# Splitting projection weights on VectorE instead of GpSimd during the delta rule, and the output residual in half rows

## The chip, the cores and the metric

The kernel runs on one core of a Trainium2 chip. The metric is the device time of one execution in microseconds (us), of which the median of several executions is taken. The profile writes PE for TensorE's matmuls and PEld for its weight loads, DVE for VectorE, ACT for ScalarE, POOL for GpSimd and SP for the engine that issues most DMAs.

## The reference, cut to what matters

One layer of a streaming encoder. A prompt of 2048 tokens and a sample of 32 tokens are normalised, projected by one wide matrix, and go through two branches:

```python
hp = layer_norm(x_prompt, ln0_g, ln0_b)                 # 2048 x 1024; the sample has 32 rows
qa, ka, va, za, qkv_b, zb, a_b, b_b, gate_a, gate_b = split_projection(hp @ w_in)
ya = (chunk_band_attention(qa, ka, va, rel_bias) * silu(za)) @ w_branch_a
ob, s_new = gated_delta_rule(q, k, v, g, beta, s0)      # after a conv of qkv_b, chunks of 64 tokens
yb = (rmsnorm(ob) * gdn_norm_w * silu(zb)) @ w_branch_b
mix = sigmoid(gate_a) * ya + sigmoid(gate_b) * yb
y = layer_norm(ALPHA * hp + mix @ w_out, ln_g, ln_b)
```

All values are fp32. To get nearly fp32 results out of fp16 matmuls, the kernel splits each operand into a high part (rounded to fp16) and a low part (what the rounding left over), and adds up three products: high by high, high by low, low by high. The change concerns where the low parts of `w_in` are formed, and the term `ALPHA * hp` of the last line, the residual.

## The kernel before, in words

**Stages.** The tokens go through in two halves of 1024 (the second with the 32 sample rows). For each half the wide projection is cut into 49 jobs of 128 columns each. A job's weights are 1024 x 128, in SBUF as a 128x1024 tile `wraw`. The first jobs of a half feed branch B, the delta rule; the following ones feed branch A, the attention. After the second half comes the merge: branch matmuls (`a<-ghi,whi` and its two companions in the profile), the gates `sg`, the output projection (`pj<-woh,mh`, `b<-woh,mh`), the residual tile `xt` and the last norm. In the profiled execution the delta rule's recurrence runs from about 217 to 510 us and again from about 1013 to 1307 us; the merge fills the time from 1661 us to the end.

**Who sets the order.** The program is written by generators ("streams") that a small planner runs in order of a planned clock: class `Flow` gives each instruction a price, and whichever stream has the earliest clock writes its next instruction. The result is one fixed list of instructions for each engine, which the chip works off in that order; an instruction that waits holds back all behind it on its engine. `flow.spend(key, cost)` moves a stream's clock on, and charges an engine's planned time, without an instruction. A price that differs from the real duration changes no instruction, only where it stands.

**A weight job.** `fetch` loads `wraw` (two buffers, `raw_gate`). `divide` (below, in `trunk`) makes the two fp16 tiles `whi` and `wlo` (two buffers each, `w_gate`). In half 0 it first finds a power of two that scales the weights: ACT squares the tile into `whi` and sums it into `w_sq`; PE adds that up over partitions (`b<-w_sq,tiny`); DVE, POOL (a `pow`) and DVE turn it into `w_scale`. In both halves ACT then writes the scaled weights back into `wraw` (`wraw<-wraw,w_scale`, 128x1024), casts them to `whi` in two halves of 512, and POOL forms `wlo` as the difference `wlo<-wraw,whi`, in two instructions of 512. `multiply` then runs 48 matmuls for a job in half 0 (two blocks of 8 x 3) and 72 in half 1: `pj<-hi,whi`, `pj<-hi,wlo`, `pj<-lo,whi`.

**The delta rule.** DVE is the engine with the most instructions here. `substitute` inverts triangular systems step by step in pairs of small instructions, `sys_t` and `sys_u`, two systems at a time. `chain` carries the state from chunk to chunk: PE `x<-state,k_bd`, DVE `r`, PE `x<-r,u_bd`, DVE `vn`, PE `x<-vn,kd_bd`, DVE `state`, two token blocks at a time. `conv` does the width-4 convolution as three `acc<-raw,cwT,acc` instructions of 128x512 on DVE. Their matmuls stand on PE between the `pj` matmuls of the weight jobs.

**The order of the jobs** is made by `all_jobs`: `HEAD` gate jobs, the job "ab", the list `ORDER` (16 jobs of branch B with 5 gate jobs between them), `TAIL` = 6 gate jobs, 16 jobs of branch A, and the remaining gate jobs.

**The merge.** PE is the bound: for each 256 tokens 16 branch products go through three `a` banks; DVE multiplies each with its gate (`sg<-sg,a`), adds pairs (`sg<-sg`), ACT makes the high part `mh`, DVE or POOL the low part `ml`, and the output projection follows. `x_load` prepares the residual of each 128 rows, `finish` adds the projection to it (`xt<-pj,xt`, `xt<-b,xt`), takes the statistics and applies the norm (`xt<-xt,m,lng`, `xt<-xt,m,lnb`). `x_load` first makes (x - mean) * rstd on DVE (`xt<-xt,mv`, 128x1024), then multiplies by the row `l0g` and adds the row `l0b` (128x1024 each), on DVE for the first two tiles and on POOL for the other fifteen.

Of the kernel before, what the change touches and what calls it, by code (L numbers as in the profile page):

```python
# [15 lines left out]
AF = mybir.ActivationFunctionType  # L16
ALU = mybir.AluOpType
# [32 lines left out]
HEAD, TAIL = [2, 3], [6, 6]  # L50
# [5 lines left out]
ORDER = [(0, 0), (0, 1), (0, 2), None]  # L56
# [212 lines left out]
def trunk(ctx: ExitStack, tc: tile.TileContext, x_p, x_s, cache_k, cache_v, st_conv, st_gdn,  # L269
          ln0_g, ln0_b, w_in, w_ab, rel_rev, conv_w, a_log, dt_bias, gdn_w, w_a, w_b, w_out,  # L270
          ln_g, ln_b, y_p, y_s, nk_p, nv_p, nc_p, ng_p, nk_s, nv_s, nc_s, ng_s):
    nc = tc.nc
    ctx.enter_context(tc.manual_schedule())
    flow = Flow()
    V = Engine(flow, nc.vector, "V")
    S = Engine(flow, nc.scalar, "S")
    G = Engine(flow, nc.gpsimd, "G")
# [3 lines left out]
    def dma(dst, src, eng=nc.sync):  # L281

        eng.dma_start(dst, src)  # L283
        size = 2 if dst.dtype == F16 else 4
        n = size
        for k in dst.shape:
            n *= k

        n = max(n, n // (size * dst.shape[-1]) * 768)
        return flow.transfer("SP" if eng is nc.sync else "S", n)  # L290
# [7 lines left out]
    def mark():  # L298
        return Mark(flow)
# [55 lines left out]
    mv = const.tile([P, SEQ // P + 1, 2], F32, name="mv")  # L355
# [215 lines left out]
    class Job:  # L571
# [3 lines left out]
        def __init__(self, half, wid, src, evac=None, key=None, cols=P, blocks=None):  # L575
            self.wid = wid
            self.half, self.src, self.evac, self.cols, self.key = half, src, evac, cols, key
            self.end = self.two = False
            self.blocks = blocks or BLOCKS[half]

    NRAW = 2
# [33 lines left out]
    def factors(wid):  # L615

        inv, half_ = w_inv[:, wid:wid + 1], w_half[:, wid:wid + 1]
        V.reciprocal(out=half_, in_=w_scale[:, wid:wid + 1])
        yield
        V.tensor_scalar(out=inv, in0=half_, scalar1=h_scale[:, 2:3], scalar2=None, op0=ALU.mult)  # L620
        V.tensor_scalar(out=half_, in0=half_, scalar1=h_scale[:, 3:4], scalar2=None, op0=ALU.mult)

    def divide():

        while True:
            job, raw, t = yield from q_raw.get()
            yield w_gate
            hi = wpool.tile([P, KD, P], F16, tag="whi", bufs=2, name="whi")
            lo = wpool.tile([P, KD, P], F16, tag="wlo", bufs=2, name="wlo")
            sc = w_scale[:, job.wid:job.wid + 1]  # L630
            yield t
            if job.half == 0:
                S.activation(out=hi[:], in_=raw[:], func=AF.Square, accum_out=w_sq[:])
                yield
                yield from power(sc, w_sq[:])
                flow.start(factors(job.wid))
            src, main = raw[:, :, 0:job.cols], hi[:, :, 0:job.cols]
            S.activation(out=src, in_=src, func=AF.Copy, scale=sc)
            for i in range(2):
                ks = slice(4 * i, 4 * i + 4)  # L640
                S.copy(out=main[:, ks], in_=src[:, ks])
                yield

                rest_ = lo[:, ks] if job.cols == P else hi[:, ks, job.cols:P]
                G.tensor_tensor(out=rest_, in0=src[:, ks], in1=main[:, ks], op=ALU.subtract)
                if i:
                    raw_gate.give()
                    q_w.put((job, hi, lo))
                yield
# [129 lines left out]

    rest = [[job_gate(half, br, f) for br in range(2) for f in range(KD)] for half in range(2)]  # L780
# [1138 lines left out]

    def all_jobs():  # L1920
        for half in range(2):
            for what in [None] * HEAD[half] + ["ab"] + ORDER:
                if what is None:
                    yield rest[half].pop(0)
                elif what == "ab":
                    yield Job(half, 48, [(0, w_ab[:, :, 0:NH]), (32, w_ab[:, :, NH:2 * NH])], key=(1, None, 0), cols=HD,
                              blocks=AB_BLOCKS[half])
                else:
                    p, i = what
                    wid = (16 + 4 * i if i < 3 else 28) + p  # L1930
                    yield Job(half, wid, [(0, w_in[wid])], key=(1, p, i))
            for _ in range(TAIL[half]):
                yield rest[half].pop(0)
            for p in range(NP):
                for i, f in enumerate((8, 4, 0, 12)):
                    yield Job(half, f + p, [(0, w_in[f + p])], key=(0, p, i))
            yield from rest[half]

    def marked():

        ahead, half = [], None
        for job in all_jobs():
            if job.half != half:
                if ahead:
                    ahead[-2].two = ahead[-1].end = True
# [12 lines left out]
        ahead[-2].two = ahead[-1].end = True  # L1958
        yield from ahead
# [200 lines left out]
    def x_ahead():  # L2160
        n = SEQ // P
        for gt in [*range(n - 2), n, n - 2, n - 1]:
            yield x_slots
            w = Rows()
            flow.start(x_load(w, gt, P if gt < SEQ // P else DEC))
            q_x[gt == SEQ // P].put(w)

    def x_load(w, gt, rows):
        w.ready, w.half_done = mark(), mark()
        w.xt = xt = fp.tile([P, D], F32, tag="xt", bufs=3, name="xt")  # L2170
        w.st = fp.tile([P, 2, 6], F32, tag="fst", bufs=3, name="fst")
        yield dma(xt[:rows], x_s if rows < P else x_p[gt * P:(gt + 1) * P, :])
        yield rows_ready
        V.tensor_scalar(out=xt[:rows], in0=xt[:rows], scalar1=mv[:rows, gt, 0:1],
                        scalar2=mv[:rows, gt, 1:2], op0=ALU.subtract, op1=ALU.mult)
        yield
        eng = V if gt < 2 else G
        eng.tensor_tensor(out=xt[:rows], in0=xt[:rows], in1=rowv["l0g"][:rows], op=ALU.mult)
        yield
        eng.tensor_tensor(out=xt[:rows], in0=xt[:rows], in1=rowv["l0b"][:rows], op=ALU.add)  # L2180
        w.ready.done()

    def finish(w, gt, rows, c, ps, end):
# [81 lines left out]
    rowv = {}  # L2265
# [42 lines left out]
```

## Time and profile before

| | us |
|---|---|
| median of 3 runs (lowest, highest) | 2088.36 (2082.26, 2091.96) |
| the profiled execution, its own time | 2083.65 |
| its span, first to last instruction | 2081.6 |
| PE busy in it | 1968.6 |
| DVE, ACT, POOL busy in it | 1499.7, 978.1, 633.1 |

The profiled execution is one run; its time is 4.7 us below the median of the three. Busy time of PE is an upper figure, since its matmuls are pipelined and their records overlap: a busy PE can still hold short waits. The rows of a group read: line, engine, operation, output<-inputs, shape, count | busy us, mean ns | idle time of the engine just before them, and what ended it. Nearly all instructions carry line 260, the helper that records them, so groups are told apart by the names of their tiles. A wait row reads: who waited <- for whom: us in total, times, longest.

### The profile page before, as it was taken

The numbers are of one execution on the slowest core, as the hardware profiler recorded it, in microseconds if no ns is written. First come the engines' busy times: TensorE is split into PE (matmuls) and PEld (weight loads), VectorE is DVE, ScalarE is ACT, GpSimd is POOL, SyncE is SP. The second block draws the span as 40 slices with busy tenths as digits, with TensorE's granted clock in tenths as the row PEclk, the third lists the DMA queues.
The fourth block names the chain that finished last, engine by engine and source line by source line (L and its number), as shares of the span: only waits on it lengthen the run. The fifth ranks groups of instructions, "written<-read, shape, count | busy, mean of one in ns | idle before, by whom it ended". The sixth has DMA issues, their size and how long they took to land. (4 is left out here: it accounts for less than half of the span.)

```text
span 2081.6 us, 41386 instructions
## 1 busy us (share of the span) xinstructions
PE 1968.6 (95%) x15098; PEld 1411.3 (68%) x15098; DVE 1499.7 (72%) x4661; ACT 978.1 (47%) x2098; POOL 633.1 (30%) x708
## 2 busy tenths in 40 slices
PE   4999999999999999998999999999999988999998
PEld 3454666766465657566667777667666777888996
DVE  7679889873377758679998986356656667666775
ACT  5565554444466667564544543355656641111110
POOL 6244333422312113243332331311011134433342
PEclk9999999999999999999999999999999999999999
DMA  3233232323423233122233233332232445433331
GB/s 119 72 92 106 75 102 57 100 80 91 116 86 111 70 92 100 65 85 72 66 89 83 77 99 84 105 92 76 72 88 88 129 137 175 132 102 122 102 116 54
DMA packets 197719, 196.49 MB, mean 94 GB/s; under 512 B 79622, under 2 KB 147570, under 8 KB 197516
## 3 DMA queue, kind: packets, MB, share of 16 engines
q1 hardware_dynamic: 197516, 193.85, 31.6%
q8 instruction: 119, 1.95, 0.4%
q14 instruction: 84, 0.69, 0.1%
HBM read 135.91 MB, written 50.53 MB: 90 GB/s over the span
## 5 line engine op out<-in xcount | busy, mean ns | idle before, releaser
L260 PE MATMUL pj<-hi,whi 128*128 128x512 f16 (+2 forms) x1992 | 644.8, 339 | 10.4 <-DVE zb L260 2.7
L260 PE MATMUL pj<-hi,wlo 128*128 128x512 f16 (+2 forms) x1952 | 635.9, 338 | 2.4 <-POOL wlo L260 2.3
L260 PEld LDWEIGHTS <-whi 128*128 128x128 f16 x3984 | 413.5, 105 | 214.5 <-issue 3.9
L260 PE MATMUL pj<-lo,whi 128*128 128x512 f16 (+2 forms) x1992 | 457.7, 340 | 0.0
L260 POOL TENSOR_TENSOR wlo<-wraw,whi 128x512 f16<-128x512 f32 x192 | 226.9, 1184 | 585.9 <-ACT whi L260 313.0
L260 PEld LDWEIGHTS <-wlo 128*128 128x128 f16 x1952 | 204.8, 105 | 111.1 <-issue 10.7
L260 ACT CAST mh<-sg 128x256 fp32r<-128x256 f32 x64 | 25.9, 406 | 279.6 <-DVE sg L260 279.6
L260 ACT CAST ph<-b 128x512 f16<-128x512 f32 (+2 forms) x224 | 93.1, 421 | 100.0 <-PE b L260 96.8
L260 DVE TENSOR_TENSOR pl<-b,ph 128x512 f16<-128x512 f32 (+2 forms) x224 | 107.7, 485 | 44.7 <-ACT ph L260 43.1
L260 PE MATMUL a<-ghi,whi 128*128 128x256 f32 (+1 forms) x512 | 132.6, 290 | 6.3 <-DVE sg L260 6.2
L260 DVE TENSOR_TENSOR sys_u<-sys_u,sys_t 128x60 f32<-128x60 f32 (+23 forms) x527 | 129.3, 251 | 6.7
L260 ACT ACTIVATE wraw<-wraw,w_scale 128x1024 f32<-128x1024 f32 (+1 forms) x98 | 111.5, 1138 | 46.6 <-DVE w_scale L260 42.9
L260 PE MATMUL a<-ghi,wlo 128*128 128x256 f32 (+1 forms) x512 | 130.3, 285 | 0.0
L260 ACT CAST whi<-wraw 128x512 f16<-128x512 f32 (+1 forms) x196 | 119.4, 612 | 20.9 <-PE pj L260 18.0
L260 DVE TENSOR_TENSOR sys_t<-sys_u,sys_p 128x60 f32<-128x60 f32 (+21 forms) x459 | 121.2, 265 | 6.1
L260 ACT ACTIVATE sb<-sb,mx,unit 128x640 f32<-128x640 f32 (+4 forms) x128 | 108.8, 851 | 20.0 <-DVE mx L260 19.7
L260 DVE SCALAR_TENSOR_TENSOR acc<-raw,cwT,acc 128x512 f32<-128x512 f32 x144 | 114.0, 792 | 5.4 <-ACT acc L260 4.4
L260 POOL TENSOR_TENSOR w_scale<-w_scale,mhalf 128x1 f32<-128x1 f32 x49 | 30.9, 631 | 269.3 <-DVE w_scale L260 204.2
L260 PE MATMUL b<-ident,sb 128*128 128x128 f32 x560 | 100.6, 279 | 5.3 <-ACT sb L260 2.2
L260 PEld LDWEIGHTS a<-ghi,whi 128*128 128x128 f32 x512 | 98.0, 191 | 9.0 <-DVE sg L260 7.8
L260 ACT COPY v_t<-o 128x64 f32<-128x64 f32 x132 | 27.7, 210 | 161.1 <-PE o L260 133.3
L260 PEld LDWEIGHTS a<-ghi,wlo 128*128 128x128 f32 x512 | 97.8, 191 | 0.3
(350 smaller groups left out, 4221.8 us busy)
## 6 DMA issues: line engine op xcount, KB each, us to landing
wraw<-in_w_in SPq DMA_DIRECT2D x192, 256.0 KB
sg<-sig SPq DMA_DIRECT2D x112, 128.0 KB
sig<-sig SPq DMA_DIRECT2D x44, 256.0 KB
sys_p<-sol_p SPq DMA_DIRECT2D x17, 512.0 KB
x<-in_x_p SPq DMA_DIRECT2D x16, 512.0 KB
xt<-in_x_p SPq DMA_DIRECT2D x16, 512.0 KB
out_y_p<-xt SPq DMA_DIRECT2D x16, 512.0 KB
glo<-g SPq DMA_DIRECT2D x14, 512.0 KB
```

The source lines that it names most:

```text
L260: r = f(*a, **k)
```

## The change

Jobs that run beside the delta rule get a mark, `delta`: all of `ORDER` and the first four of the six `TAIL` jobs in both halves, and the `HEAD` jobs of half 1: 25 jobs in half 0 and 28 in half 1, 53 of 96 with low parts. For them

- ACT no longer writes the scaled weights back. It makes each half of `whi` straight from the raw weights, with the scale (`whi<-wraw,w_scale`, 512);
- DVE forms the low part from the raw weights, `wlo = wraw * w_scale - whi`, in one instruction for each half, in place of POOL. The instruction is written past the planner's own wrapper, and its 0.7 us are charged to a key "W" which no engine has, so that the plan sees DVE as free;
- in half 0 the stream waits 1.0 us of planned time between ACT's square and the matmul of `w_sq`.

The other jobs keep the old way. In the merge, all residual tiles are done by DVE: (x - mean) * l0g, then that * rstd + l0b, each in two halves of 512 columns; POOL has none of them left.

```diff
             if job.half == 0:
                 S.activation(out=hi[:], in_=raw[:], func=AF.Square, accum_out=w_sq[:])
-                yield
+
+                yield flow.cur.clock + (1.0 if job.delta else 0.0)
                 yield from power(sc, w_sq[:])
                 flow.start(factors(job.wid))
             src, main = raw[:, :, 0:job.cols], hi[:, :, 0:job.cols]
-            S.activation(out=src, in_=src, func=AF.Copy, scale=sc)
+            if not job.delta:
+                S.activation(out=src, in_=src, func=AF.Copy, scale=sc)
             for i in range(2):
                 ks = slice(4 * i, 4 * i + 4)
-                S.copy(out=main[:, ks], in_=src[:, ks])
-                yield
 
                 rest_ = lo[:, ks] if job.cols == P else hi[:, ks, job.cols:P]
-                G.tensor_tensor(out=rest_, in0=src[:, ks], in1=main[:, ks], op=ALU.subtract)
+                if job.delta:
+
+                    S.activation(out=main[:, ks], in_=src[:, ks], func=AF.Copy, scale=sc)
+                    yield
+                    nc.vector.scalar_tensor_tensor(out=rest_, in0=src[:, ks], scalar=sc, in1=main[:, ks],
+                                                   op0=ALU.mult, op1=ALU.subtract)
+                    flow.spend("W", 0.7)
+                else:
+                    S.copy(out=main[:, ks], in_=src[:, ks])
+                    yield
+                    G.tensor_tensor(out=rest_, in0=src[:, ks], in1=main[:, ks], op=ALU.subtract)
...
-        V.tensor_scalar(out=xt[:rows], in0=xt[:rows], scalar1=mv[:rows, gt, 0:1],
-                        scalar2=mv[:rows, gt, 1:2], op0=ALU.subtract, op1=ALU.mult)
-        yield
-        eng = V if gt < 2 else G
-        eng.tensor_tensor(out=xt[:rows], in0=xt[:rows], in1=rowv["l0g"][:rows], op=ALU.mult)
-        yield
-        eng.tensor_tensor(out=xt[:rows], in0=xt[:rows], in1=rowv["l0b"][:rows], op=ALU.add)
+        for name, q, op0, op1 in (("l0g", 0, ALU.subtract, ALU.mult), ("l0b", 1, ALU.mult, ALU.add)):
+            for c in range(2):
+                cs = slice(c * 512, (c + 1) * 512)
+                V.scalar_tensor_tensor(out=xt[:rows, cs], in0=xt[:rows, cs], scalar=mv[:rows, gt, q:q + 1],
+                                       in1=rowv[name][:rows, cs], op0=op0, op1=op1)
+                yield
```

(The part left out gives the jobs in `all_jobs` their mark, and sets it to False when a job is made.)

Since the planner's clock moves, every engine's list is written anew: PE's has as many matmuls of each kind as before, in another order. Three places show what that means.

DVE in the delta rule of the second half, where a conv ends (`acc`, `qk_s`) beside two systems (`sys_t`, `sys_u`) and the state chain (`r`, `vn`, `state`). Before:

```order
L260 TENSOR_SCALAR vn<-x,sc 128x64
L260 TENSOR_TENSOR sys_u<-sys_u,sys_t 128x2x24
L260 TENSOR_TENSOR sys_u<-sys_u,sys_t 128x8
L260 SCALAR_TENSOR_TENSOR qk_s<-e,acc 128x32
L260 SCALAR_TENSOR_TENSOR state<-state,sc,x 128x64
L260 TENSOR_TENSOR sys_t<-sys_u,sys_p 128x3x23
L260 TENSOR_TENSOR sys_u<-sys_u,sys_t 128x3x23
L260 SCALAR_TENSOR_TENSOR acc<-raw_14016,cwT,acc 128x512
L260 SCALAR_TENSOR_TENSOR r<-x,negc,v_t_10362 128x64
```

The same place in the changed kernel:

```order
L260 SCALAR_TENSOR_TENSOR qk_s<-e,acc 128x32
L260 SCALAR_TENSOR_TENSOR state<-state,sc,x 128x64
L260 TENSOR_TENSOR sys_t<-sys_u,sys_p 128x2x24
L260 TENSOR_TENSOR sys_t<-sys_u,sys_p 128x7x5
L649 SCALAR_TENSOR_TENSOR wlo<-wraw,w_scale,whi 128x512
L260 TENSOR_TENSOR sys_u<-sys_u,sys_t 128x2x24
L260 TENSOR_TENSOR sys_u<-sys_u,sys_t 128x7x5
L260 SCALAR_TENSOR_TENSOR r<-x,negc,v_t_10335 128x64
```

A low part now stands in DVE's list between a state step and the next `r`; nothing else was taken out there to make room.

PE in the delta rule of the first half, at a matmul of `w_sq` among the products `b<-qk,k_bd` that begin a token block. Before:

```order
L260 MATMUL b<-w_sq,tiny 128x1
L260 LDWEIGHTS whi
L260 MATMUL pj<-hi_150,whi 128x512
L260 MATMUL b<-qk_1403,k_bd_580 128x128
L260 LDWEIGHTS wlo
L260 MATMUL pj<-hi_150,wlo 128x512
```

Now:

```order
L260 MATMUL b<-qk_1375,k_bd_580 128x128
L260 LDWEIGHTS whi
L260 MATMUL pj<-hi_150,whi 128x512
L260 MATMUL b<-qk_1375,k_bd_580 128x128
L260 LDWEIGHTS wlo
L260 MATMUL pj<-hi_150,wlo 128x512
L260 MATMUL b<-w_sq,tiny 128x1
```

The `w_sq` matmul, which waits for ACT's square, stands behind several products now that it stood ahead of.

DVE at the start of the merge's residual tiles, when the first outputs come. Before:

```order
L260 TENSOR_SCALAR xt<-xt,mv 128x1024
L260 SCALAR_TENSOR_TENSOR xt<-pj,xt 128x512
L260 SCALAR_TENSOR_TENSOR xt<-b,xt 128x512
L260 TENSOR_TENSOR xt<-xt,l0g 128x1024
L260 BN_STATS fst<-xt 128x6
```

Now:

```order
L260 SCALAR_TENSOR_TENSOR xt<-xt,mv,l0g 128x512 x2
L260 SCALAR_TENSOR_TENSOR xt<-xt,mv,l0b 128x512 x2
L260 SCALAR_TENSOR_TENSOR xt<-xt,mv,l0g 128x512
L260 SCALAR_TENSOR_TENSOR xt<-pj,xt 128x512
L260 SCALAR_TENSOR_TENSOR xt<-b,xt 128x512
```

The whole-row steps are gone, and half-row steps stand in their place; POOL's list has no `xt` row any more.

More of the change, by code (lines that the diff above doesn't have):

```diff
@@ L577, in __init__ @@
             self.half, self.src, self.evac, self.cols, self.key = half, src, evac, cols, key
-            self.end = self.two = False
+            self.end = self.two = self.delta = False
             self.blocks = blocks or BLOCKS[half]
@@ L1921, in all_jobs @@
         for half in range(2):
-            for what in [None] * HEAD[half] + ["ab"] + ORDER:
+            for n, what in enumerate([None] * HEAD[half] + ["ab"] + ORDER):
                 if what is None:
-                    yield rest[half].pop(0)
+                    job = rest[half].pop(0)
+                    job.delta = half == 1 or n >= HEAD[0]
+                    yield job
                 elif what == "ab":
@@ L1930, in all_jobs @@
                     wid = (16 + 4 * i if i < 3 else 28) + p
-                    yield Job(half, wid, [(0, w_in[wid])], key=(1, p, i))
-            for _ in range(TAIL[half]):
-                yield rest[half].pop(0)
+                    job = Job(half, wid, [(0, w_in[wid])], key=(1, p, i))
+                    job.delta = True
+                    yield job
+            for n in range(TAIL[half]):
+                job = rest[half].pop(0)
+                job.delta = n < TAIL[half] - 2
+                yield job
             for p in range(NP):
```

## The prediction, written before the changed kernel ran

> **What bounds the kernel now.** I read the page first, then a table of stages, and then who waits for whom inside the stages that the change touches.
>
> ```profile
> PE 1968.6 (95%) x15098; PEld 1411.3 (68%) x15098; DVE 1499.7 (72%) x4661; ACT 978.1 (47%) x2098; POOL 633.1 (30%) x708
> ```
>
> PE is busy nearly all the time, so only what makes PE wait counts. By stages (columns: PE, PEld, DVE, ACT, POOL busy, granted clock, DMA) the two delta rules and the steady merge read:
>
> ```profile
> 208.00:468.00 260.00, 245.67 (x1904) 167.26 (x1903) 222.44 (x850) 126.85 (x265) 90.71 (x111) 0.98 0.31 83
> 936.00:1300.00 364.00, 343.10 (x3013) 257.80 (x3011) 316.61 (x1158) 166.46 (x380) 114.08 (x158) 0.99 0.31 81
> 1768.00:2028.00 260.00, 258.25 (x1624) 233.31 (x1623) 177.59 (x284) 33.47 (x93) 100.63 (x80) 1.00 0.36 114
> ```
>
> In the delta rules DVE is busy 222.44 of 260 and 316.61 of 364 us (86 and 87%): second in line behind PE, with 85 us idle in the two together. In the merge PE leaves 1.75 us of 260. What PE waits for in the delta rules, first half and then second:
>
> ```profile
> PE x L260 <- DVE r L260: 5.6, 6, 2.3
> PE x L260 <- DVE state L260: 2.6, 5, 0.9
> PE x L260 <- DVE vn L260: 2.4, 4, 0.9
> ...
> PE x L260 <- DVE r L260: 9.0, 11, 1.4
> PE x L260 <- DVE state L260: 2.2, 5, 0.8
> PE x L260 <- DVE vn L260: 1.3, 4, 0.6
> ```
>
> These are 10.6 and 12.5 us, 23.1 together: the state chain on DVE, late. That is the size of what is at stake there.
>
> **Part 1: POOL's low parts stop holding DVE.** The timeline shows how POOL reaches PE, at one place of the second delta rule:
>
> ```profile
> 1248.02 2.27 POOL L260 TENSOR_TENSOR wlo<-wraw,whi 128x512 f16<-128x512 f32 x2
> 1249.27 1.08 DVE L260 TENSOR_TENSOR sys_u<-sys_u,sys_t 128x48 f32<-128x48 f32 x1
> 1250.76 0.28 DVE L260 SCALAR_TENSOR_TENSOR r<-x,negc,v_t 128x64 f32<-128x64 f32 x1
> 1251.09 0.43 PE L260 MATMUL x<-r,u_bd 128*128 128x64 f32 x2 [1.43 <-DVE r L260]
> ```
>
> A small DVE instruction that starts while POOL's `wlo` runs ends just after it, 1.08 us instead of 0.2; `r` follows late, and PE idles 1.43 us. How much of this there is, by the mean of the system steps (groups) against their median (tile), first half and then second:
>
> ```profile
> L260 DVE TENSOR_TENSOR sys_u<-sys_u,sys_t 128x60 f32<-128x60 f32 (+23 forms) x188 | 43.8, 240 | 2.1
> L260 DVE TENSOR_TENSOR sys_t<-sys_u,sys_p 128x8 f32<-128x8 f32 (+15 forms) x163 | 42.6, 264 | 2.0
> ...
> L260 DVE TENSOR_TENSOR sys_u<-sys_u,sys_t x188: 147/209/1143, 208.0 to 466.8; 128x60 f32<-128x60 f32 x18, 128x28 f32<-128x28 f32 x12, 128x54 f32<-128x54 f32 x12, 128x48 f32<-128x48 f32 x12
> L260 DVE TENSOR_TENSOR sys_t<-sys_u,sys_p x163: 130/214/1191, 208.2 to 464.8; 128x60 f32<-128x60 f32 x18, 128x54 f32<-128x54 f32 x12, 128x48 f32<-128x48 f32 x12, 128x66 f32<-128x66 f32 x12
> ...
> L260 DVE TENSOR_TENSOR sys_u<-sys_u,sys_t 128x54 f32<-128x54 f32 (+23 forms) x279 | 71.2, 260 | 3.6
> L260 DVE TENSOR_TENSOR sys_t<-sys_u,sys_p 128x60 f32<-128x60 f32 (+21 forms) x243 | 63.3, 261 | 3.2
> ...
> L260 DVE TENSOR_TENSOR sys_u<-sys_u,sys_t x279: 156/214/1221, 938.1 to 1279.9; 128x60 f32<-128x60 f32 x12, 128x54 f32<-128x54 f32 x10, 128x66 f32<-128x66 f32 x9, 128x28 f32<-128x28 f32 x8
> L260 DVE TENSOR_TENSOR sys_t<-sys_u,sys_p x243: 155/217/1224, 942.7 to 1279.7; 128x60 f32<-128x60 f32 x12, 128x54 f32<-128x54 f32 x10, 128x66 f32<-128x66 f32 x9, 128x48 f32<-128x48 f32 x7
> ```
>
> First half 188 x 31 + 163 x 50 ns = 14.0 us, second 279 x 46 + 243 x 44 ns = 23.5 us: 37.5 us of DVE time. Not all of it is `wlo`, since POOL does other work too: by its share of POOL's time (below, 33.05 of 90.71 and 44.52 of 114.08) it would be 14 us; but `wlo` is POOL's long instruction, so I take 28.
>
> **Part 2: DVE takes the low parts on.** The stages have these low parts (the same windows, of the `wlo` instructions alone), and the nearest instruction with two SBUF inputs, a scalar from a tile and 512 columns is the conv's:
>
> ```profile
> 208.00:468.00 260.00, 82.27 (x215) 25.80 (x215) 0.00 (x0) 33.05 (x28) 0.98 0.31 83
> 936.00:1300.00 364.00, 136.34 (x457) 50.59 (x458) 0.00 (x0) 44.52 (x38) 0.99 0.31 81
> ...
> L260 DVE SCALAR_TENSOR_TENSOR acc<-raw,cwT,acc x144: 711/744/1698, 87.4 to 1175.4; 128x512 f32<-128x512 f32 x144
> ```
>
> All 28 of the first move, and 36 of the second (one of its 19 jobs is a late `TAIL` job): 64 x 0.744 = 47.6 us on DVE. Against 28 us given back, DVE gets 19.6 us more work into 85 us of idle time. How much of a DVE delay reaches PE? At least nothing; at most all. PE's waits of 23.1 us against 37.5 us of lengthening and all ordinary queueing say less than 0.6; I choose 0.3, for both parts: 0.3 x (47.6 - 28) = +6 us. The other 42 new instructions lie outside these windows, where DVE has room: nothing, with that idle time as the cover.
>
> A wait is added: DVE's list now waits for ACT's `whi`, and behind it stand `r`, `vn` and `state`, for which PE waits. POOL waited long there (first row below), being early; DVE works through a backlog. The nearest row of DVE waiting for an ACT cast is the attention's (second row): 0.65 us in 66 of 224 cases. I take nothing, and keep that for the rivals.
>
> ```profile
> POOL wlo L260 <- ACT whi L260: 328.3, 131, 14.0
> DVE pl L260 <- ACT ph L260: 43.1, 66, 1.5
> L260 ACT ACTIVATE wraw<-wraw,w_scale 128x1024 f32<-128x1024 f32 (+1 forms) x98 | 111.5, 1138 | 46.6 <-DVE w_scale L260 42.9
> ```
>
> ACT loses 53 instructions of 1.138 us, 60 us; PE hardly waits for ACT in the delta rule, so I give this -2 us (0 to -4). In SP's list some weight loads move ahead of the transfers of the systems (`sol_p`, `gcb`), since `wraw` is planned free sooner; each such place costs those one or two issues, by the row
>
> ```profile
> L283 SPq DMA_DIRECT2D wraw<-in_w_in x192: 327/423/1431, 3.3 to 1597.1; - x192
> ```
>
> 0.42 us each, and the systems are read well before PE needs them: nothing.
>
> A rule that bears on part 1 is the Trainium skill's, SBUF — State Buffer, section "Who interferes with whom": VectorE instructions with two SBUF inputs and GpSimd instructions that read SBUF exclude each other for a whole instruction. By that rule the new instructions can also be held by POOL's remaining work, 57.7 of 260 and 69.6 of 364 us here, about 20% of 64 starts at half a microsecond, 6 us on DVE and 2 at PE, which would make the sum 2 us worse; the timeline above agrees with the rule.
>
> **Part 3: the matmul of `w_sq` later.** In half 0 PE reaches it before ACT's square is done (52 to 520 us):
>
> ```profile
> L260 PE MATMUL b<-w_sq,tiny 128*128 128x1 f32 x58 | 10.1, 244 | 5.0 <-ACT whi L260 3.9 <-DVE kd_bd L260 1.2
> L260 PEld LDWEIGHTS b<-w_sq,tiny 128*128 128x128 f32 x58 | 9.3, 189 | 13.0 <-ACT whi L260 11.0 <-issue 1.6
> ```
>
> A microsecond later in the plan most of it is covered: between the two rows, -6 us (0 to -11). The job's chain gets 1.0 us longer by this and shorter by ACT's 1.14 us.
>
> **Part 4: the residual in the merge.** DVE's groups from 1768 us on, the waits from 1700 us on, and the residual's durations:
>
> ```profile
> L260 DVE TENSOR_TENSOR sg<-sg 128x256 f32<-128x256 f32 x41 | 44.1, 1076 | 0.7
> L260 DVE SCALAR_TENSOR_TENSOR sg<-sg,a 128x256 f32<-128x256 f32 x81 | 32.4, 413 | 10.7 <-PE a L260 9.2 <-DMA sg<-sig 1.5
> ...
> PE a L260 <- DVE sg L260: 6.2, 6, 2.1
> ...
> L260 DVE TENSOR_SCALAR xt<-xt,mv x17: 793/806/817, 1730.9 to 2032.7; 128x1024 f32<-128x1024 f32 x16, 32x1024 f32<-32x1024 f32 x1
> L260 DVE SCALAR_TENSOR_TENSOR xt<-xt,m,lng x17: 1261/1277/2844, 1743.9 to 2075.2; 128x1024 f32<-128x1024 f32 x16, 32x1024 f32<-32x1024 f32 x1
> L260 POOL TENSOR_TENSOR xt<-xt,l0g x15: 2389/2395/2518, 1738.9 to 2034.3; 128x1024 f32<-128x1024 f32 x14, 32x1024 f32<-32x1024 f32 x1
> ```
>
> The same 256 columns take 1.076 us from two SBUF tiles and 0.413 with one in PSUM: 41 x 0.66 = 27 us that POOL's `xt` costs DVE. New on DVE: 17 x 4 x 0.744 = 50.6 us, less 17 x 0.806 = 13.7, so +37; net +10 in a stage where DVE idles a third. PE's `a` products wait 6.2 us in all for `sg`; with the long holds gone I take -4 (0 to -6).
>
> One rule speaks against the halves: the Trainium skill, VectorE: DVE Perf Modes, "Rules for kernel authors", says to keep the number of DVE instructions low. By rows, two whole-row steps would be 2 x 1.277 = 2.55 us a tile against 2.98, 7 us over 17 tiles; in a stage with idle DVE that makes the sum 1 us better at most.
>
> **The sum.** +6 - 2 - 6 - 4 = -6 us. The profiled execution took 2083.65, so 2077.65; the median is 4.7 higher, 2088.36 - 6 = 2082. The order is written anew everywhere, which I count as +-6 us.
>
> **The rivals.**
> 1. *DVE becomes the bound of the delta rule* (slower). 64 waits of 0.65 us for ACT (41.6) join 47.6 us of work, and half of it reaches PE: 0.5 x (89.2 - 28) = +31, with -12 elsewhere +19: 2107 us. For it: 87% busy, and a plan that thinks DVE free. Against: idle time of 85 us, and 23.1 us of waits. From a share of 0.37 on it is over 0.5%, which is about what a measurement of this kernel can tell from no change. Chance 0.19.
> 2. *The holds did most of the harm* (much faster). The lengthened instructions are long and hit chains, the new ones fall in gaps: -0.5 x 28 + 0.1 x 47.6 - 6 - 2 - 4 = -21: 2067 us. For it: the timeline above. Against: a low part of 0.74 us delays `r` as surely. Chance 0.27.
> 3. The forecast or near it: 0.54. That the change isn't made is excluded by the order, which has 106 `wlo` rows on DVE and no `xt` row on POOL.
>
> **How the numbers follow.** Around -6 with +-8, the forecast is faster by over 10.4 us (0.5%) in 0.25 of its cases, same in 0.7, slower in 0.05; rival 2 is faster in 0.85, rival 1 slower in 0.8. Faster 0.54 x 0.25 + 0.27 x 0.85 = 0.36, slower 0.18, same 0.46. The range reaches to rival 2 and a little beyond and most of the way to rival 1: 2064 to 2102.
>
> **What would show it.** Right: system steps near their median of 0.21 us in the delta rules; PE's waits for `r`, `vn`, `state` still near 20 us; hardly any idle time before `w_sq`; `sg<-sg` near 0.42 us. Wrong: those waits for the chain at 35 us or more, with DVE above 95% busy there or waiting for `whi` (rival 1), or at 10 or less (rival 2).

## The result, and the profile after

| | us |
|---|---|
| kernel before, median of 9 runs (lowest, highest) | 2087.93 (2077.27, 2091.96) |
| changed kernel, median of 9 runs (lowest, highest) | 2099.53 (2090.55, 2104.16) |
| ratio, 95% interval | 1.0056 (1.0042, 1.0070) |

The changed kernel is slower by 11.6 us, where 6 us less had been forecast. The time lies inside the range; the sign does not. The profiled execution of it took 2104.16 us, 4.6 above its median, and that of before 4.3 below its own, so some 9 of the 20.5 us between the two traces are spread of single runs. Much of that spread goes with TensorE's granted clock: of the nine runs of the changed kernel the shortest (2090.55 us) had a mean clock of 0.987, the longest, which is the profiled one, 0.977; the profiled execution of before had 0.988. The verdicts below therefore go by ratios, and the traces say where.

First what the prediction said would show. The stages of after, for the same windows as before (PE, PEld, DVE, ACT, POOL busy, granted clock, DMA):

```profile
208.00:468.00 260.00, 243.01 (x1839) 167.39 (x1838) 215.89 (x846) 111.88 (x246) 58.39 (x82) 0.96 0.31 83
936.00:1300.00 364.00, 348.98 (x2949) 259.66 (x2947) 320.01 (x1174) 156.28 (x363) 71.97 (x130) 0.98 0.31 84
1768.00:2028.00 260.00, 257.91 (x1684) 236.38 (x1683) 173.84 (x334) 35.69 (x96) 46.27 (x59) 1.00 0.39 121
```

POOL is relieved as intended, and DVE is about as busy in these windows as before (215.89 and 320.01 against 222.44 and 316.61), though it has the low parts now. The second delta rule starts 37 us later in after, so its window does not hold the same work; the groups and waits of after that follow are therefore taken from 208 to 540 and from 936 to 1350 us, which hold the whole of each. The groups show why DVE is no busier:

```profile
L260 DVE TENSOR_TENSOR sys_u<-sys_u,sys_t 128x60 f32<-128x60 f32 (+22 forms) x200 | 42.3, 218 | 2.1
L260 DVE TENSOR_TENSOR sys_t<-sys_u,sys_p 128x60 f32<-128x60 f32 (+12 forms) x175 | 37.4, 218 | 2.0
...
L260 DVE TENSOR_TENSOR sys_u<-sys_u,sys_t 128x66 f32<-128x66 f32 (+24 forms) x279 | 60.6, 221 | 3.4
L260 DVE TENSOR_TENSOR sys_t<-sys_u,sys_p 128x60 f32<-128x60 f32 (+20 forms) x243 | 51.8, 214 | 2.6
```

The means of 240 to 264 ns fell to 214 to 221, about the median of before (209 to 217): POOL's low parts had caused nearly all of the lengthening. PE's waits for the state chain in after, first and second delta rule, come to 13.0 and 7.3 us, 20.3 together, near the 20 forecast:

```profile
PE x L260 <- DVE r L260: 5.2, 10, 1.4
PE x L260 <- DVE vn L260: 5.1, 8, 2.7
PE x L260 <- DVE state L260: 2.7, 3, 1.7
...
PE x L260 <- DVE r L260: 5.3, 11, 0.8
PE x L260 <- DVE vn L260: 1.6, 4, 0.8
PE x L260 <- DVE state L260: 0.4, 2, 0.3
```

The matmul of `w_sq` (52 to 520 us) waits 0.4 us where it had waited 5.0, and the pair sums of the merge take 424 ns where they had taken 1076:

```profile
L260 PE MATMUL b<-w_sq,tiny 128*128 128x1 f32 x56 | 8.3, 218 | 0.4 <-DVE ss L260 0.4
...
L260 DVE TENSOR_TENSOR sg<-sg 128x256 f32<-128x256 f32 (+1 forms) x56 | 23.8, 424 | 0.5
```

All four signs of "right" are there, and the kernel is slower. So the loss is at places that the forecast did not look at. The first and last start of two kinds of matmul show where: the attention's scores of the first half, and the state products of the second. In before:

```profile
L260 PE MATMUL a<-kst,ql x96: 219/299/380, 567.5 to 797.3; 128*128 128x320 f16 x64, 128*128 128x128 f16 x8, 128*128 128x256 f16 x8, 128*128 128x384 f16 x8
...
L260 PE MATMUL x<-vn,kd_bd x136: 219/275/324, 1012.6 to 1307.4; 128*128 128x64 f32 x136
```

In after:

```profile
L260 PE MATMUL a<-kst,ql x96: 219/299/380, 581.9 to 812.3; 128*128 128x320 f16 x64, 128*128 128x128 f16 x8, 128*128 128x256 f16 x8, 128*128 128x384 f16 x8
...
L260 PE MATMUL x<-vn,kd_bd x136: 218/275/422, 1049.5 to 1341.1; 128*128 128x64 f32 x136
```

The first half is 14 us late at its scores (567.5 to 581.9). Between the last score and the second delta rule 215.3 us became 237.2: 22 us more. The second delta rule itself is 3.2 us shorter (294.8, now 291.6). The timeline of after shows where the 22 us begin:

```profile
863.99 0.71 ACT L260 ACTIVATE whi<-wraw,w_scale 128x512 f16<-128x512 f32 x1
...
865.73 0.38 PE L260 MATMUL pj<-hi,whi 128*128 128x512 f16 x1
...
866.46 0.91 DVE L260 MEMSET qk_bd<- 128x1024 f32 x1 [0.16 <-issue]
...
876.12 0.91 DVE L260 MEMSET u_bd<- 128x1024 f32 x1 [0.16 <-issue]
876.96 1.28 DVE L649 SCALAR_TENSOR_TENSOR wlo<-wraw,w_scale,whi 128x512 f16<-128x512 f32 x2
...
877.64 0.61 PE L260 MATMUL pj<-hi,wlo 128*128 128x512 f16 x1 [11.53 <-DVE wlo L649]
```

ACT has `whi` ready by 864.7, but DVE forms `wlo` only at 876.96: ahead of it in DVE's list stand the 17 memsets of 128x1024 that clear the second half's block-diagonal tiles (`diag`), one every 1.07 us, written into the list in one piece. The next product in PE's list needs it, and PE waits 11.53 us. It is the third of the three `HEAD` jobs of the second half. In the kernel before, POOL made that low part, and these memsets did not stand in its way.

After the wait the clock is at half. Windows of 3.4 us in after (the granted clock is the third figure from the end):

```profile
866.60:870.00 3.40, 0.00 (x0) 0.00 (x0) 2.91 (x4) 0.83 (x2) 0.67 (x1) 1.00 0.13 41
...
873.40:876.80 3.40, 0.00 (x0) 0.00 (x0) 2.92 (x4) 0.00 (x0) 0.00 (x0) 0.50 0.00 0
...
880.20:883.60 3.40, 3.40 (x10) 1.16 (x9) 0.00 (x0) 0.00 (x0) 0.00 (x0) 0.50 0.21 78
```

From 877.64 to 883.6 us PE works again, but at 0.50: another 3 us lost.

That is not all that the clock costs. The mean granted clock of the whole trace is 0.977 against 0.988 in before. Since the clock is either at 1.00 or at 0.50 in these windows, that is an estimated 97 us at half speed against 50, and only some 14 us of the difference lie at this wait. The rest is spread over the kernel, much of it in the first half (a mean of 0.96 up to 570 us, against 0.99 in before). A run below shows that this part need not come from the order of the instructions.

### The profile page after: what moved, and what is told of

Its sections match the earlier page's. It is cut to its first block, busy times and chain, and to the rows that moved or that the text cites. A ratio compares the mean times of both kernels' runs of the same rounds, so it can differ in the third digit from the quotient of the medians.

```text
span 2102.0 us, 41351 instructions
## 1 busy us (share of the span) xinstructions
PE 1976.6 (94%) x15098; PEld 1420.8 (68%) x15098; DVE 1492.0 (71%) x4814; ACT 934.5 (44%) x2045; POOL 434.3 (21%) x572
## 5 line engine op out<-in xcount | busy, mean ns | idle before, releaser
L260 PE MATMUL pj<-hi,wlo 128*128 128x512 f16 (+2 forms) x1952 | 641.4, 341 | 14.3 <-DVE wlo L649 11.5
L260 POOL TENSOR_TENSOR wlo<-wraw,whi 128x512 f16<-128x512 f32 x86 | 99.8, 1164 | 348.6 <-issue 198.6
L260 DVE TENSOR_TENSOR sys_u<-sys_u,sys_t 128x60 f32<-128x60 f32 (+23 forms) x527 | 113.2, 219 | 6.3
L260 DVE SCALAR_TENSOR_TENSOR acc<-raw,cwT,acc 128x512 f32<-128x512 f32 x144 | 107.6, 747 | 6.1 <-ACT acc L260 5.0
L260 DVE TENSOR_TENSOR sys_t<-sys_u,sys_p 128x60 f32<-128x60 f32 (+20 forms) x459 | 97.9, 216 | 5.3
L260 ACT ACTIVATE whi<-wraw,w_scale 128x512 f16<-128x512 f32 x106 | 75.4, 717 | 56.5 <-DVE w_scale L260 35.3
L260 DVE CUSTOM_DVE_ANT_0 sb<-a,bias 128x320 f32<-128x320 f32 (+4 forms) x128 | 61.4, 485 | 46.7 <-PE a L260 45.9
```

Source lines behind the costliest of these rows:

```text
L260: r = f(*a, **k)
```

## The experiments

Theory A: the loss is this one wait with the slow clock behind it; the merge is a gain. Theory B, the prediction's rival 1 (DVE becomes the bound of the delta rule): the low parts load DVE in the delta rules, and that passes on to PE. Theory C: the new order of the first half and its 1.0 us of delay cost the time. Each ratio is to the kernel before, run on the same chip, with its 95% interval; a difference of two ratios has the root of the summed squares of their half widths, and 0.001 is 2.1 us.

**Merge alone.** The kernel before with the last piece of the diff, the residual in halves, and nothing else.

> The kernel before with the new residual in halves alone, no low part on DVE. Theory A (the loss is one wait: TensorE's 11.7 us for a gate job's low part that stands behind DVE's 17 memsets between the halves; the merge is a gain): 6 to 10 us below the kernel before, ratio 0.995 to 0.997, since the merge stretch took 411 us in the changed kernel and 420.6 in the kernel before. Theory B (the low parts load DVE in the delta rules and that passes on to TensorE): the same, it says nothing of the merge. If the merge's gain of 9.6 us was only what another order of jobs left over, the ratio is 1.000.

Ratio 0.9950 (0.9934, 0.9965), 2075.31 us: a gain of 10.4 us, the upper end of what was expected.

**Low parts alone.** The changed kernel with the old residual.

> The changed kernel with the old residual in the merge: the low parts on DVE alone. Theory A: the wait of 11.7 us between the halves is there again, with the slow clock behind it, and the merge's gain is gone: 16 to 22 us above the kernel before, ratio 1.008 to 1.010. Theory B: the same total, but spread over the two delta rules as waits for r, vn and state, 26 us and more in each instead of the 13.0 and 7.3 us seen in the changed kernel.

Ratio 1.0080 (1.0057, 1.0104), 2102.82 us. The wait was there again, 13.2 us long, and PE's waits for `r`, `vn` and `state` were 10.6 and 7.6 us in the two delta rules, not the 26 and more of theory B. So the low parts' half of the change is the slow one.

**Without the head jobs.** The three gate jobs at the head of the second half take their low part from POOL:

```diff
-                    job.delta = half == 1 or n >= HEAD[0]
+                    job.delta = n >= HEAD[half]
```

> The changed kernel, but the three gate jobs at the head of the second half take their low part from POOL as before; all other low parts stay on DVE. Theory A: the wait of 11.7 us at about 866 us goes and the stretch from the end of the first scores to the second delta rule falls from 237 us back to 215 to 220: 12 to 20 us below the changed kernel, ratio 0.996 to 1.000 to the kernel before. Theory B: 3 jobs of 106 change little, ratio 1.004 to 1.006 as with the changed kernel. Theory C (the new order and the 1.0 us wait of a job in the first half cost the 17 us seen by its end): the wait goes but the total stays at 1.003 or above.

Ratio 0.9962 (0.9945, 0.9978), 2077.87 us: 0.0094 +- 0.0022 or 19.6 us less than the changed kernel, by moving 6 of its 106 low parts. The longest wait of PE between 820 and 905 us is now

```profile
PE pj L260 <- ACT hi L260: 1.4, 1, 1.4
```

Theory B can't explain that: 100 low parts are still on DVE. Theory C as the whole of the loss (1.003 or above) falls too.

This run also tells how far the stages of single traces can be trusted. PE's list is the same as in the changed kernel up to the head jobs of the second half, yet the scores of the first half start at 571.1 us in this trace and at 581.9 in that of the changed kernel. The mean granted clock up to 570 us was 0.98 here and 0.96 there. With low parts alone (above) and with the memsets on POOL (below) the list is the same too, and the scores start at 579.4 and 581.0 us, with a clock of 0.96. So of the 14 us by which the changed kernel was late at its scores 3.6 are left in the best of these traces; the other 10.8 go with the clock, which differs between executions of one list.

**Memsets on POOL.** The changed kernel with the memsets of the second half written for POOL, so that DVE's list is free:

```diff
-                V.memset(t[:], 0.0)
+                (G if half else V).memset(t[:], 0.0)
```

> The changed kernel with the 17 memsets that clear the second half's block-diagonal tiles on POOL, so that no low part on DVE stands behind them. Theory A: DVE forms the gate job's low part at once, TensorE doesn't wait there, and the time is within 4 us of the run with the three gate jobs on POOL, unless the ab job's low part, which POOL forms and which stands behind the memsets there, is now what TensorE waits for (then some 5 to 12 us of the wait stay). Theory B: ratio 1.004 to 1.006 as with the changed kernel, since the load of the delta rules is untouched.

Ratio 0.9993 (0.9974, 1.0011), 2084.14 us. The wait for `wlo` is gone here too, with all 106 low parts on DVE; 13 of the 20 us are back. The other 6.5 us (0.0031 +- 0.0025 above the run without the head jobs, where at most 4 had been expected) were not found as one wait: between 820 and 905 us PE waits 2.2 us for `hi`, 2.8 for `tmp` and 1.3 for `ga`, against 1.4, 0.4 and nothing in the run without the head jobs, so it is probably a number of short waits in the order that the head jobs bring; that is not shown. The ab job, at which the expectation had looked, held PE for 0.8 us only, as in the changed kernel.

**The head jobs alone.** Merge, and only these three jobs on DVE.

```diff
-                    job.delta = half == 1 or n >= HEAD[0]
+                    job.delta = half == 1 and n < HEAD[1]
...
-                    job.delta = True
+                    job.delta = False
```

> The kernel before with the new residual, and of the 53 marked jobs the three gate jobs at the head of the second half alone: 6 low parts on DVE instead of 106. The third job's low part stands behind the 17 memsets as in the changed kernel. Theory A: these 6 instructions carry the loss; against the run with the merge alone (ratio 0.995, 2075.3 us) 14 to 22 us longer, ratio 1.002 to 1.006 to the kernel before, with one wait of 10 to 14 us for `wlo`. Theory B (the load of the 106 low parts): next to nothing is left of the loss, ratio 0.995 to 0.997.

Ratio 1.0052 (1.0033, 1.0071), 2097.64 us: 21 us above the merge alone, from six instructions. PE's waits between 820 and 905 us begin with

```profile
PE pj L260 <- DVE wlo L649: 13.2, 1, 13.2
```

Theory A holds for this part, from both sides. But the merge alone was at 0.9950 and the run without the head jobs at 0.9962: the other 100 low parts seemed worth nothing. The next runs take the halves apart.

**Second half alone**, without head jobs; the first half as before.

> The changed kernel with low parts on DVE in the second half alone, without its three head jobs; the first half as before, without its 1.0 us. In the run without the head jobs the second delta rule was about 5 us shorter than with POOL's low parts (290.1 against 295.5 us from the first to the last state product), so theory A expects 3 to 6 us below the merge alone: 2069 to 2073 us, ratio 0.992 to 0.994, the best of all. Theory B: the low parts cost in either delta rule, ratio 0.996 or above. Theory C (only the first half's order costs): as theory A.

Ratio 0.9898 (0.9880, 0.9916), 2067.36 us: 10.8 us (0.0052 +- 0.0024) below the merge alone, more than expected. The stage of the second delta rule and its groups, in the merge alone:

```profile
936.00:1300.00 364.00, 343.33 (x2990) 257.39 (x2989) 315.56 (x1154) 165.96 (x378) 114.09 (x158) 0.98 0.30 81
```

```profile
L260 DVE TENSOR_TENSOR sys_u<-sys_u,sys_t 128x54 f32<-128x54 f32 (+23 forms) x279 | 71.1, 259 | 3.6
L260 DVE TENSOR_TENSOR sys_t<-sys_u,sys_p 128x60 f32<-128x60 f32 (+21 forms) x243 | 63.2, 261 | 3.2
...
L260 DVE SCALAR_TENSOR_TENSOR acc<-raw,cwT,acc 128x512 f32<-128x512 f32 x51 | 39.7, 779 | 0.2
```

With the low parts of this half on DVE:

```profile
936.00:1300.00 364.00, 348.10 (x3054) 262.46 (x3053) 307.77 (x1186) 152.15 (x362) 73.14 (x118) 0.99 0.31 84
```

```profile
L260 DVE TENSOR_TENSOR sys_u<-sys_u,sys_t 128x66 f32<-128x66 f32 (+24 forms) x274 | 59.6, 221 | 3.3
L260 DVE TENSOR_TENSOR sys_t<-sys_u,sys_p 128x54 f32<-128x54 f32 (+21 forms) x241 | 51.3, 214 | 2.6
...
L649 DVE SCALAR_TENSOR_TENSOR wlo<-wraw,w_scale,whi 128x512 f16<-128x512 f32 x36 | 27.1, 752 | 0.0
```

27.1 us of new work, and DVE's busy time falls by 7.8, so the rest of its work takes some 35 us less. The shorter system steps are 22 us of that (279 x 38 + 243 x 47 ns) and the shorter `acc` 2 us; the remainder is not taken apart, and part of it is that the window does not hold quite the same instructions (274 and 48 against 279 and 51 in the first and third rows). PE got through more of its list in the same stretch (3054 matmul records, not 2990), and its wait for `r` fell from 9.0 to 5.6 us. That is the prediction's rival 2 (the holds did most of the harm).

**First half alone**, with the 1.0 us of delay.

> The changed kernel with low parts on DVE in the first half alone. Without the head jobs the first half took about 4 us more up to the first state product (221.7 against 217.2 us) and nothing after it. Theory A and theory C: 2 to 6 us above the merge alone, ratio 0.996 to 0.998, with the wait of PE for `p_c` at about 187 us. Theory B: 5 us and more above it, with the waits for r, vn and state grown. If it is 0.995 or below, the first half's order costs nothing and its 4 us are spread of single runs.

Ratio 1.0003 (0.9990, 1.0017), 2085.76 us: 11 us (0.0053 +- 0.0021) above the merge alone, more than expected. PE's waits for `r`, `vn` and `state` in the first delta rule hardly grew (11.9 us against 11.3 in the merge alone), though theory B needs that. So there was a second loss, in the first half, as theory C had it.

**No delay.** The run without the head jobs, and

```diff
-                yield flow.cur.clock + (1.0 if job.delta else 0.0)
+                yield
```

> The run without the head jobs, and without the 1.0 us of planned time between ACT's square and the matmul of `w_sq` in the first half. The delay was forecast to be worth 6 us: by that forecast this run is 3 to 8 us above the one with the delay (ratio 0.998 to 1.000), with the waits of the `w_sq` matmul and its weights back at 10 us or more. If the delay only moves the wait elsewhere (the wait for `p_c` at 187 us would then be its price), the time is the same or up to 4 us below, ratio 0.994 to 0.996.

Ratio 0.9903 (0.9889, 0.9917), 2066.55 us, below what either outcome allowed: the delay costs 12.3 us (0.0059 +- 0.0022). It had been forecast to bring 6, by sparing PE the wait for `w_sq`. Without it that wait and that of its weight load (52 to 520 us) are

```profile
L260 PE MATMUL b<-w_sq,tiny 128*128 128x1 f32 x58 | 9.9, 240 | 1.1 <-ACT whi L260 0.9
L260 PEld LDWEIGHTS b<-w_sq,tiny 128*128 128x128 f32 x58 | 9.7, 194 | 7.2 <-ACT whi L260 5.7 <-PE b L260 0.3 <-issue 0.3
```

1.1 us, down from 5.0, and 7.2, down from 13.0. In the second half alone, where the first half is as before and has no delay either, the wait was 5.1 us; so it is the first half's low parts that took it away, most likely since ACT is rid of its 1.14 us per job and the square comes earlier. The delay has little left to save. What it moves can be seen in SP's list. Without the delay:

```profile
167.95 1.10 SPq L283 DMA_DIRECT2D gcb<-gc_dram  x2
169.31 0.56 SPq L283 DMA_DIRECT2D sys_p<-sol_p  x1
...
177.70 0.42 SPq L283 DMA_DIRECT2D z<-zb  x1
```

With 1.0 us (the run without the head jobs):

```profile
168.21 1.10 SPq L283 DMA_DIRECT2D gcb<-gc_dram  x2
172.46 0.34 SPq L283 DMA_DIRECT2D z<-zb  x1
173.03 0.56 SPq L283 DMA_DIRECT2D sys_p<-sol_p  x1
```

The store `z<-zb` waits for DVE until 172.46 us, and the load of the next system, ready to go, waits behind it. From there the wait is handed from list to list:

```profile
184.61 0.24 DVE L260 TENSOR_SCALAR sys_t<-sys_p,sys_u 128x31 f32<-128x31 f32 x1 [3.07 <-DMA sys_p<-sol_p]
...
186.23 0.21 ACT L260 ACTIVATE sc<-sc 128x8 f32<-128x8 f32 x1 [3.54 <-DVE sc L260]
...
190.21 1.01 PE L260 MATMUL b<-sel,p_c 128*64 128x2 f32 x8 [5.00 <-ACT p_c L260]
```

DVE stops 3.07 us at the system; `sc` stands behind it, ACT waits for `sc`, and `p_c` stands behind that on ACT; PE waits 5.00 us for `p_c`.

A second store stands ahead of such a load at 258.5 us. Theory D: it is this order that costs, not the delay. Theory E: the delay itself costs. The plan writes these two stores ahead of the loads with delays of 0.7 and 1.0 us, and behind them with 0 and with 2.0.

**A delay of 2.0 us.**

> The run without the head jobs (1.0 us of delay, ratio 0.9962), with 2.0 us in place of 1.0. Without any delay it was 0.9903, so the delay costs some 12 us in the first half. Theory D (what costs is the order of SP's list that the plan happens to write: with 1.0 us a store `z<-zb` that waits for DVE stands ahead of the load `sys_p<-sol_p` twice, with 0 and with 2.0 us it stands behind it): ratio 0.989 to 0.993, as without a delay. Theory E (the delay itself costs, each microsecond more): 0.998 to 1.003.

Ratio 0.9880 (0.9856, 0.9905), 2063.34 us: the lowest ratio here, though its interval reaches over those without delay (0.9903) and of the second half alone (0.9898). Theory E falls.

**A delay of 0.7 us.**

> The same with 0.7 us of delay; SP's list has both stores `z<-zb` ahead of the loads of the systems, as with 1.0. Theory D: ratio 0.994 to 0.998, with a wait of PE for `p_c` of 4 us or more at about 187 us. Theory E: in proportion, 0.993 to 0.996, with no such wait needed.

Ratio 0.9953 (0.9935, 0.9971), 2075.76 us, as with 1.0. DVE's waits for the systems and PE's wait for `p_c` are larger still; the rows (52 to 540 us) of this run:

```profile
DVE sys_t L260 <- DMA sys_p<-sol_p: 13.0, 4, 4.3
...
PE b L260 <- ACT p_c L260: 6.6, 2, 6.1
```

**Only the two stores moved.** The 1.0 us of delay stay, all lists are word for word those of the run without the head jobs, and in SP's the two stores are issued right after the load that stood behind them:

```diff
+        if late:
+            held.append((dst, src))
+        else:
+            eng.dma_start(dst, src)
...
+                while held:
+                    nc.sync.dma_start(*held.pop())
```

> The run without the head jobs (1.0 us of delay, ratio 0.9962), with two changes of place in SP's list and nothing else: the two stores `z<-zb` of the first half that stand ahead of a load `sys_p<-sol_p` are put right behind it. All other engines' lists are the same, word for word. Theory D (the order of SP's list is the price of the delay): ratio 0.988 to 0.992, the wait of PE for `p_c` at about 187 us falls from 5 us to under 3, and DVE's waits for `sys_p` in the first half from 4.8 us to under 2. If something else in the new order costs (D falls): 0.995 to 0.997.

```profile
169.62 1.10 SPq L288 DMA_DIRECT2D gcb<-gc_dram  x2
170.96 0.56 SPq L288 DMA_DIRECT2D sys_p<-sol_p  x1
173.87 0.34 SPq L1252 DMA_DIRECT2D z<-zb  x1
```

The wait for `p_c` near 187 us fell from 5.0 to 1.8 us and DVE's waits for the systems from 4.8 to 2.3. The ratio is 0.9939 (0.9922, 0.9957), 2072.63 us: between the two outcomes. The two places are worth 5 us (0.0023 +- 0.0024) of the 12, an interval that reaches to nothing: the traces show the waits, but the price of the two stores is not shown. The other 7.5 us (0.0036 +- 0.0022, against no delay) come with the rest of the new order. From 290 to 545 us PE waits here 5.1 us for `vn`, 1.9 for `v_t`, 1.8 for `vs`, 1.3 for the square of `w_sq` and 1.1 for `tu_t`, against 3.1 for `vn`, 0.5 for the square and nothing for the others without the delay; which of them matter stays open. That it is the order, and not the length of the delay, follows from the run with 2.0 us, and from what the delay is: planned time, for which no instruction is written.

**The head jobs on DVE, known to the plan.** Without delay; the low parts of the three head jobs go through the planner's wrapper and are charged to DVE.

> The run without delay, but with the three head jobs of the second half on DVE again, their six low parts written through the planner's wrapper and charged to DVE's planned time. The third job's low part still stands behind the 17 memsets in DVE's list. Uncharged, these jobs cost 19 to 21 us (0.9903 + 0.0095 = 0.9998). Theory F (the plan not knowing is what makes PE wait): it puts other work of PE ahead of that job, and the ratio is 0.990 to 0.994. Theory G (DVE is taken for 18 us there, and PE has nothing else to do, known or not): a wait of 8 us or more for that low part or for what the job holds up, ratio 0.996 to 1.000.

Ratio 0.9982 (0.9968, 0.9997), 2082.78 us, with

```profile
PE pj L260 <- DVE wlo L260: 13.2, 1, 13.2
```

Theory G: that the plan took DVE for free is not what made PE wait. With the price known, the low part still stands behind the memsets, and the plan puts no other work of PE in the gap. The three jobs cost 16.5 us (0.0079 +- 0.0021 above no delay).

**Whole rows in the merge.** The merge alone, its two steps over 1024 columns:

> The kernel with the merge's new residual alone (ratio 0.995), but the two steps over whole rows of 1024 columns instead of halves. If the gain is that POOL no longer holds DVE there (sg<-sg at 1.076 us), the halves don't matter: ratio 0.994 to 0.996, DVE 0.4 us a tile less busy. If short instructions matter (a whole row is 1.27 us or more, and the product `a` waits for `sg`): 0.996 to 0.998, with PE's waits for `sg` back at 6 us.

Ratio 0.9943 (0.9926, 0.9961), 2074.96 us, the same as in halves. From 1768 us on:

```profile
L260 DVE TENSOR_TENSOR sg<-sg 128x256 f32<-128x256 f32 (+1 forms) x48 | 20.7, 434 | 0.4
...
L260 DVE SCALAR_TENSOR_TENSOR xt<-xt,mv,l0g 128x1024 f32<-128x1024 f32 (+1 forms) x12 | 15.3, 1277 | 0.0
```

Halving the rows brings nothing that shows. What both runs share is that POOL no longer does these rows beside DVE, and `sg<-sg` is down to 425 and 434 ns in them; that this makes the gain is likely but not shown apart, since the two steps were also fused and the order was written anew. In the merge alone PE's waits from 1700 us on fell from 6.2 to 3.4 us for `sg` and from 3.2 to 0.6 for `mh`, which is half of the 10.4 us.

## Why the prediction was wrong, point by point

The runs make a path from the kernel before to the changed one; each row is the difference of two measured ratios, times 2086 us, and is uncertain by 3 to 5 us. The rows add up to the whole by construction; in another order of steps they could come out otherwise.

| step | us measured | us forecast |
|---|---|---|
| residual in the merge (merge alone) | -10.4 | -4 |
| low parts of the second half, no head jobs (second half alone less merge alone) | -10.8 | +6 - 2 for both halves |
| low parts of the first half, no delay (no delay less second half alone) | +1 | |
| 1.0 us of delay (without head jobs less no delay) | +12.3 | -6 |
| the three head jobs (changed kernel less without head jobs) | +19.6 | 0 |
| sum | +11.7 | -6 |

- **The step that failed** is "The other 42 new instructions lie outside these windows, where DVE has room: nothing, with that idle time as the cover." Six of the 42 cost 19.6 us. Idle time elsewhere is no cover: what counts is what stands ahead of an instruction in its new engine's list at that place. Taking the 17 memsets out of DVE's list gave 13 us back; the other 6.5 stay open. The memsets were in the trace of before, 0.91 us each, and the order would have shown the low part behind them.
- **The delay** was priced by the wait that it was to save (5.0 us, and 13.0 of the weight load). That wait had mostly gone by another part of the same change. The order in SP's list was given nothing, since "the systems are read well before PE needs them", and it was the weight loads that were looked at; in the run a store stood ahead of the load, and DVE waits 3.07 us for a system, with ACT and PE behind it. These places are at most a part of the 12.3 us; the rest of the new order has the other part, and which waits in it count is open.
- **The low parts in the delta rules**: the holds were there, the way from DVE to PE was wrong. I gave POOL's `wlo` 28 of 37.5 us of lengthening for both halves; in the second half alone 22 us came back in the systems, of the 23.5 that I had counted there, and 2 in `acc`. The low parts' own price was right, 0.744 us forecast and a mean of 0.752. But I set the two against each other and let 0.3 of the difference reach PE. In the second half that difference is about 3 us more work (27.1 less 24), and yet 10.8 us were gained. Rival 2's two shares give -9.3 there, as an estimate (0.1 x 27.1 - 0.5 x 24). So rival 2 was right about the delta rules, in the second half; in the first the +1 us is uncertain by 5. Two losses outside hid it. Rival 1 gave the right sign by a mechanism that isn't there: it had 41.6 us of DVE waiting for ACT's `whi`, and the changed kernel has 0.5 us of that in the two delta rules.
- **A rule of the Trainium skill** was set beside this: SBUF — State Buffer, "Who interferes with whom", by which POOL's remaining work can hold the new two-input instructions too, 6 us on DVE by my estimate. Here the mean of 36 of them is 8 ns above the median of 744, 0.3 us in all; the direction agrees, the price was far too high.
- **The merge** was a gain of two and a half times the forecast. I had counted only PE's waits for `sg`; they fell by 2.8 us, those for `mh` by 2.6, and the other half was not found.
- **The clock** is in none of the terms. Estimated from the traces' means, PE's clock was at half for 97 us in the changed kernel and for 50 before; how much of the 11.6 us goes that way was not taken apart.

The two terms that decide the sign were put at zero and at the wrong sign. Both are about the order of the lists, not about how long an instruction takes; for the head jobs it is shown what stood ahead, for the delay only in part.

## What to carry to other kernels

When work moves to an engine with idle time, look for each place at what stands ahead of it in that engine's list, one-time work like clearing buffers above all: three jobs, one of them behind 17 memsets, cost twice what the other fifty gained in a busy stretch. A store that waits for its data, ahead of a load that is ready, held the load here for 3 us; after any change that rewrites the order, read the queue of the DMAs at the loads on which the critical chain depends. Before a difference between two traces is put down to the order, look whether the clock was the same: here one and the same list of PE reached the scores 10.8 us apart in two executions. And try the pieces of a change apart: here two of five were worth 10 us each, and the whole was a loss; the version with all low parts but those of the head jobs and another planned delay beat the kernel before by 1.2%.

## What the hardware showed that was not expected

PE's last matmul before the long wait starts at 865.73 us. The granted clock stays at 1.00 until 870.0, is 0.50 until 883.6, and so is low for the first 6 us of work after the wait: a wait of 11.5 us costs about 14.5, since 6 us at half the clock do 3 us of work. That agrees with the Trainium skill, TensorE: Matmul & The Clock Gate, "Part 1: The HAM clock gate", which gives windows of about 3.4 us, idle for the half rate and busy for the full one; here the steps lie at multiples of 3.4 us (870.0 to 883.6 is four), and work that began within one window brought the full clock only at the end of the next.
